# RWKV rebuilt: the triangular inverse as 32x32 tile products on TensorE, keys of two heads formed at 128 partitions, and the old state added by rows of ones in the state's product

## The chip, the cores and the metric

The kernel runs on one core of one Trainium2 chip. The metric is the device time of one execution in microseconds (us). The engines are TensorE (PE, with weight loads shown apart as PEld), VectorE (DVE), ScalarE (ACT) and GpSimd (POOL); SyncE (SP) issues most transfers. A view of the profile shows all of them on one time axis, from the start of the profiled span.

## What is computed

One inference step of a two-layer encoder trunk over 512 prompt tokens and 32 sample tokens, with 1024 features. Both layers have a half SwiGLU, a mixer, cross-attention to 256 memory rows, and another half SwiGLU, each followed by a norm. Layer 0 mixes with a gated linear recurrence and retention, layer 1 with RWKV-7, which is what the change touches: 16 heads of 64, each with a 64x64 state.

```python
def mixer_c(x, shift_buf, s0, mu, w_rkv, w0, w1, w2, a0, a1, a2, g1, g2, k_k, k_a, r_k, gn_g, gn_b, w_out):
    ...
    r, k, v = rkv[0], rkv[1], rkv[2]
    w = -jax.nn.softplus(-(w0 + jnp.tanh(xm[3] @ w1) @ w2)) - 0.5
    decay = jnp.exp(-jnp.exp(w.astype(f32)))
    iclr = jax.nn.sigmoid(a0 + (xm[4] @ a1) @ a2)
    g = jax.nn.sigmoid(xm[5] @ g1) @ g2
    ...
    kk = k * k_k.reshape(RWKV_HEADS, RWKV_HEAD)
    kk = kk / jnp.maximum(jnp.linalg.norm(kk, axis=-1, keepdims=True), 1e-12)
    k = k * (1.0 + (iclr - 1.0) * k_a.reshape(RWKV_HEADS, RWKV_HEAD))

    def step(S, inp):
        r_t, w_t, k_t, v_t, kk_t, b_t = inp
        sa = jnp.einsum('bhvk,bhk->bhv', S, -kk_t)
        S = S * w_t[:, :, None, :] + sa[..., None] * b_t[:, :, None, :] + v_t[..., None] * k_t[:, :, None, :]
        return S, jnp.einsum('bhvk,bhk->bhv', S, r_t)
    ...
    o = layer_norm(o, gn_g..., gn_b..., RWKV_GN_EPS)
    o = o + (r * k * r_k).sum(-1, keepdims=True) * v
    y = (o.reshape(B, T, D).astype(x.dtype) * g) @ w_out
```

## The kernel before

**Layout and linear work.** The whole trunk is one program. Activations lie with features on partitions and tokens in columns, in two halves: A is tokens 0 to 255 of the prompt (256 columns), B is tokens 256 to 511 and the 32 sample tokens (288 columns). Weights stream in as granules of 128 outputs by 8x128 inputs. Each is split into a high part (a copy on ACT) and a low part (a difference on DVE or POOL), and a half's columns are split likewise; a linear granule is then 24 TensorE products of 128x256 or 128x288 (high by high, low by high, high by low). In the trace their operands are called XHA, XLA, HHA, HLA and the same with B for columns, and `W_k` for a slot of split weights, `wr` for a buffer that a load lands in.

**The order of the work.** The parts of the model are Python generators, the tasks. A planner, `Clock`, keeps an estimate of when each engine is free and each operand written. Every helper that issues an instruction (`mm` for a product, `tr` for a transpose, `tt`, `stt`, `_v` for DVE, `gtt` for POOL, `act` for ACT) names a cost to it, and the estimated start becomes the instruction's priority in the scheduler that fixes every engine's queue. `ett` picks the engine, DVE or POOL, that is through first by that estimate. So the numbers in the helpers set the order of the whole program, and no engine's queue is reordered once it is built. A list `SOLO` lets half A run ahead around RWKV, so that A's recurrence stands beside the projections of B, and B's beside A's attention and SwiGLU. A task's band (-1 to -4) puts it ahead of other work.

**The RWKV stage.** `wkv` works on 9 blocks of 64 tokens: four of half A, four of half B and one of 32 sample tokens. A block has two chunks of 32 tokens, the last block one: 17 chunks. Five tasks run side by side.

- `wkv_prep` (band -1) forms per block the decays, the keys and their inverse-decayed forms, then for each chunk and head the product KL'X, 64x64, whose masked result lies in rows 64 to 127 of X. X holds receptance and normalised key (two kinds of 32 columns), KL key and gated key. Both are built for each parity of heads at 64 partitions. The strict triangle N of each head is in X's last 32 rows. The first product of each block's keys is the one with `bonest` 128x512.
- `wkv_solve` (band -2) makes (I + N)^-1 for the 32 heads-and-chunks of a block. N goes by DMA from X to DRAM (`dn<-XHA`, `dn<-W`, one for each chunk) and from there to a tile with one head, chunk and quarter of the rows on each partition (`P<-dn`). Z (part of tile `LC`) starts as the identity; 31 steps of two POOL products each, `P<-LC,P` and `LC<-LC,P`, run on it. Z goes back by DMA (`dz<-LC`, then `W<-dz`) as four-head block-diagonal 128x128 tiles, TB.
- `wkv_load` (band -3) turns KL to tokens-first rows and loads the values' rows into Y.
- `wkv_chain` (band -4) is the recurrence: 16 products over 96 rows, 64 columns (`ax<-wr,W 96*32`), a copy, four products with TB 128x64, copies into Y, 16 products 64x64 of the tokens-first keys with Y, and then on DVE the sum with the old state and the product with the decay; beside it 16 output products of 32 columns (`ax<-XLA,wr 128*64`).
- `wkv_norm` (band -1) is the heads' norm, the bonus and the gate, with four POOL products per block.

The state, DMA staging and scratch live in room that others have left: units of X and KL in the slots XHA, XLA, two weight slots `W_110`/`W_111`, Q1 and P0; N and the step's scratch in P1 (`P_115` in the order, `P` in the profile), TB in a third weight slot (`W_114`). PSUM gives the stage five banks: two to the chain (`ax`), one to load and norm, and two (`pb`, named `mm`) to prep.

The solve's steps, and the end of the chain's state product:

```python
        for s in range(31):
            nr, nt = s // 4 + 1, 31 - s
            T = w.t[:, :nr * nt].rearrange("p (i t) -> p i t", i=nr)
            K.gtt(T, Z[:, :nr, s:s + 1].to_broadcast([128, nr, nt]), N[:, s:s + 1, s + 1:].to_broadcast([128, nr, nt]))
            K.gtt(Z[:, :nr, s + 1:], Z[:, :nr, s + 1:], T, ALU.subtract)
```

## Time and profile before

| | |
|---|---|
| Median of 3 runs | 3024.68 us (3018.31 to 3030.01) |
| Span of the profiled execution | 3028.7 us; the page gives no separate device time for it |
| Granted TensorE clock, mean | 0.945 |
| PE busy | 2833.4 us (94%), 22456 instructions |
| DVE busy | 1743.4 us (58%), 3099 |
| ACT busy | 1276.8 us (42%), 2184 |
| POOL busy | 830.1 us (27%), 1088 |
| Read from HBM | 313.09 MB, 108 GB/s over the span |
| First product of block 0's keys | 1855.97 us |
| End of chunk 7 (half A) and chunk 16 (last) | about 2157 and 2512 us |

How to read it: the share of busy time is a mean over stages with different limits, so the prediction reads it in windows cut at the stage's borders. PE's time includes time at a lowered clock; the windows give the granted clock beside it. One instruction of the program that multiplies in full fp32 leaves two matmul records and two weight loads in the trace, a linear one (in the rounded format) one of each. The chain of waits follows the end of the program back through whatever was waited for last. In a group's row the text before the bar is the operation with its output and inputs and the count, behind it the busy time and the mean of one instruction in ns, then the idle time just before these and what ended it.

### The profile page before, as it was taken

To read this page: it belongs to the slowest core of one execution; us is meant where nothing else is said; L and a number is where in the kernel's file an instruction comes from. 1 tells how busy PE (TensorE), PEld (TensorE's weight loads), DVE (VectorE), ACT (ScalarE), POOL (GpSimd) and SP (SyncE) were. 2 spreads that over 40 slices of the span, in tenths; PEclk is the share of its full clock that TensorE was granted. 3 is DMA by queue.
4 is the path that set the end of the run, shared out by engine and by line. 5 is a ranking of instruction groups with operands and counts; after the bars stand their busy time and mean duration, and the time that the engine had idled before them with its cause. 6 is when DMAs were issued, how large, how long until landed. Compare 5 with 4: busy or idle time off the path is not lost.

```text
span 3028.7 us, 54637 instructions
## 1 busy us (share of the span) xinstructions
PE 2833.4 (94%) x22456; PEld 2716.3 (90%) x22456; DVE 1743.4 (58%) x3099; ACT 1276.8 (42%) x2184; POOL 830.1 (27%) x1088
## 2 busy tenths in 40 slices
PE   9999998998999999999999898888878889999998
PEld 8999998998998999989999897776767779998997
DVE  5333337677767333365355756674675666767655
ACT  4223233665545222234244343343435455655544
POOL 2001104333313000032011212466375543422301
PEclk9999999999999999999999998788778879999999
DMA  6443443322332232322356453122223135645563
GB/s 182 126 119 115 130 119 97 88 68 81 98 98 84 85 90 84 89 87 77 90 155 179 120 168 106 39 65 62 69 73 87 49 98 174 177 141 157 169 176 93
DMA packets 626331, 330.56 MB, mean 109 GB/s; under 512 B 45480, under 2 KB 620160, under 8 KB 626080
## 3 DMA queue, kind: packets, MB, share of 16 engines
q1 hardware_dynamic: 617952, 317.06, 36.8%
q0 software_dynamic: 3488, 9.44, 1.0%
q8 instruction: 176, 2.88, 0.4%
q10 hardware_dynamic: 4640, 0.56, 0.1%
q14 instruction: 75, 0.61, 0.1%
HBM read 313.09 MB, written 13.92 MB: 108 GB/s over the span
## 4 chain that ended last, share of the span: by engine, by line
PE 66%; DVE 10%; POOL 9%; DMA 7%; ACT 5%; issue 3%; SPq 0%; ACTq 0%; DVEq 0%; POOLq 0%
PE mm L395 60%; PE ax L395 4%; POOL LC L412 3%; POOL P L412 3%; DMA P<-dn 3%; DVE W L408 2%; ACT arena L486 1%; ACT W L486 1%; DVE arena L408 1%; DMA wr<-in_ffn_up 1%; PE ax L400 1%; DVE arena L432 1%; POOL arena L412 1%; ACT L2049 1%; DVE XB L408 1%
## 5 line engine op out<-in xcount | busy, mean ns | idle before, releaser
L486 ACT ACTIVATE W<-wr 128x1024 fp32r<-128x1024 f32 (+1 forms) x558 | 577.0, 1038 | 737.4 <-PE mm L395 560.0
L408 DVE TENSOR_TENSOR W<-wr,W 128x1024 fp32r<-128x1024 f32 (+1 forms) x455 | 561.5, 1236 | 551.7 <-ACT W L486 542.8
L395 PE MATMUL mm<-XHB,W 128*128 128x288 f32 x3840 | 585.1, 302 | 14.1 <-ACT XHB L486 4.7
L395 PE MATMUL mm<-XHA,W 128*128 128x256 f32 x3840 | 538.4, 290 | 28.9 <-ACT XHA L486 11.6
L395 PEld LDWEIGHTS mm<-XHB,W 128*128 128x128 f32 x3840 | 532.4, 191 | 25.0 <-ACT XHB L486 5.8
L395 PEld LDWEIGHTS mm<-XHA,W 128*128 128x128 f32 x3840 | 499.7, 194 | 39.7 <-ACT XHA L486 16.0
L412 POOL TENSOR_TENSOR W<-wr,W 128x1024 fp32r<-128x1024 f32 (+1 forms) x103 | 251.0, 2439 | 606.2 <-ACT W L486 550.6
L395 PE MATMUL mm<-XLB,W 128*128 128x288 f32 x1984 | 318.7, 300 | 0.7 <-DVE XLB L408 0.7
L395 PE MATMUL mm<-HHB,W 128*128 128x288 f32 x1920 | 291.0, 301 | 11.4 <-ACT W L486 4.4
L395 PEld LDWEIGHTS mm<-XLB,W 128*128 128x128 f32 x1984 | 283.0, 190 | 3.2 <-DVE XLB L408 1.1
L395 PE MATMUL mm<-XLA,W 128*128 128x256 f32 x1984 | 284.7, 283 | 0.0
L395 PEld LDWEIGHTS mm<-HHB,W 128*128 128x128 f32 x1920 | 267.0, 191 | 15.0 <-ACT W L486 5.3
L395 PE MATMUL mm<-HHA,W 128*128 128x256 f32 x1920 | 265.7, 288 | 5.9 <-POOL W L412 2.2
L395 PEld LDWEIGHTS mm<-XLA,W 128*128 128x128 f32 x1984 | 259.1, 190 | 0.3 <-DVE XLA L408 0.2
L395 PEld LDWEIGHTS mm<-HHA,W 128*128 128x128 f32 x1920 | 247.1, 192 | 8.8 <-POOL W L412 2.6
L486 ACT ACTIVATE arena<-mm 128x256 f32<-128x256 f32 (+4 forms) x292 | 112.2, 387 | 305.1 <-PE mm L395 287.5
L432 DVE SCALAR_TENSOR_TENSOR arena<-mm,arena 128x288 f32<-128x288 f32 (+1 forms) x176 | 77.2, 439 | 157.7 <-PE mm L395 149.0
L395 PE MATMUL mm<-HLB,W 128*128 128x288 f32 x896 | 144.3, 301 | 0.3 <-DVE HLB L408 0.3
L412 POOL TENSOR_TENSOR P<-LC,P 128x66 f32<-128x66 f32 (+24 forms) x279 | 113.5, 407 | 84.6 <-DMA P<-dn 64.6
L395 PEld LDWEIGHTS mm<-HLB,W 128*128 128x128 f32 x896 | 130.1, 193 | 0.6 <-DVE HLB L408 0.5
L395 PE MATMUL mm<-HLA,W 128*128 128x256 f32 x896 | 129.3, 284 | 0.0
L412 POOL TENSOR_TENSOR LC<-LC,P 128x66 f32<-128x66 f32 (+24 forms) x279 | 115.0, 412 | 20.5
(426 smaller groups left out, 3612.0 us busy)
## 6 DMA issues: line engine op xcount, KB each, us to landing
wr<-in_ffn_up SPq DMA_DIRECT2D x246, 512.0 KB
wr<-in_ffn_down SPq DMA_DIRECT2D x96, 448.0 KB
wr<-in_l_w_rkv SPq DMA_DIRECT2D x48, 512.0 KB
wr<-in_ffn_down SPq DMA_DIRECT2D x40, 512.0 KB
wr<-in_l_w_in SPq DMA_DIRECT2D x24, 512.0 KB
wr<-in_l_w_out SPq DMA_DIRECT2D x24, 512.0 KB
wr<-in_xa_q SPq DMA_DIRECT2D x24, 512.0 KB
wr<-in_xa_o SPq DMA_DIRECT2D x24, 512.0 KB
```

The source lines that it names most:

```text
L395: self.nc.tensor.matmul(out, lhsT, rhs, start=start, stop=stop)
L400: self.nc.tensor.transpose(out, in_, self.ident[k0:k0 + k, k0:k0 + k])
L408: self.nc.vector.tensor_tensor(out, a, b, op=op)
L412: self.nc.gpsimd.tensor_tensor(out, a, b, op=op)
L432: self.nc.vector.scalar_tensor_tensor(out, a, s, b, op0=op0, op1=op1)
L486: return self.nc.scalar.activation(out, a, f, bias=bias, scale=scale, **kw)
L2049: nc.scalar.preload_act_table_set(name)
```

## The change

- **Inverse.** `wkv_solve` no longer uses POOL and DRAM. N is split by masks into the parts within tiles of 8 rows (d and its transpose dt), within 16 but not 8 (et) and the rest (ft). The inverse of the 8-row part is (I-d)(I+d2)(I+d4) by products, and the two larger parts are taken in by two more steps. All of it is eleven times 32 (16 in the last block) products of 32x32 by 32x32, four of them side by side in the four 32-row, 32-column quadrants of the array, with six evictions to SBUF by ACT and DVE between them. It takes its two PSUM banks from the same pair as prep (`w.ps = w.pb`). N and its transpose come from 64 products of 32x32 over 64 rows (`mm<-W 32x32 x64` below).
- **Keys.** X and KL of both chunks of a block are formed at 128 partitions at once, two heads of a pair on the two halves of the partitions. The key products run two side by side (two 64x64 quadrants). ACT copies the odd heads' keys to the lower partitions.
- **State.** The tokens-first keys have their own buffers, KT, with the identity in rows 0 to 63, so that the state's product over 128 rows adds the old state; the DVE sum goes.
- **TB** is applied as 16 products of 32x64 per chunk instead of four of 128x64, and has three buffers, so that the solve may be three blocks ahead of the chain (two before).
- **POOL to DVE.** The product with `k_k` in prep and four products and sums per block in the norm change from `gtt` to `tt`. In the norm the copy of the centred rows by ACT goes and its second PSUM bank comes from `pb`. Prep takes its two gate banks one after the other.
- **Planner.** The costs in `mm`, `_v`, `gtt`, `ett`, `gmemset`, `scan` and `act` have other numbers; `mm` has an argument `side`, how many products stand side by side. The priorities of the whole program come from these.
- Room: Q1 and P0 are given back at the start; blocks take XHA and XLA (half A), then XHB and XLB. Comments are taken out.

```diff
@@ class Kern
-    def mm(self, out, lhsT, rhs, start=True, stop=True):
+    def mm(self, out, lhsT, rhs, start=True, stop=True, side=1):
         n = free_size(rhs)
+        m = out.shape[0]
         if lhsT.dtype == F32R:
-            cost = (n if n >= 256 else max(4 * n, 128)) / 2.4 + 2
+            cost = n / 2.4 + 13 if n >= 256 else max(4 * n / 2.4, m / 1.2) + 2
+        elif m > 64 and side == 1:
+            cost = max(4 * n / 2.4, 2 * m / 1.2) + 15
         else:
-            cost = 4 * (max(n, 62) / 2.4) + 2
+            cost = (4 * n / 2.4 + 2 * m / 1.2) / side + 2
...
-        self.plan("v", 70 + free_size(out) / (1.92 if fast else 0.96), [out], ins)
+        self.plan("v", 147 + free_size(out) / (1.92 if fast else 0.96), [out], ins)
...
-        self.plan("g", 150 + free_size(out) * 2.0, [out], [a, b])
+        self.plan("g", 190 + free_size(out) * 2.1, [out], [a, b])
...
-        dur = (60 if a.space == PSUM else 100) + free_size(out) / 1.2
+        dur = (165 if a.space == PSUM else 204) + free_size(out) / 1.2
@@ wkv_norm
-        K.act(o, p3)
...
-        K.gtt(o, o, q)
-        K.gtt(o, o, bv(K.gng2))
+        K.tt(o, p3, q)
+        K.tt(o, o, bv(K.gng2))
...
@@ wkv
+    for t in w.kt:
+        K.vcopy(t[0:64], K.ident[0:64, None, 0:64].to_broadcast([64, 16, 64]))
+    K.qt.give("Q1", "P0")
...
+    w.ps = w.pb
@@ wkv_prep
-        K.gtt(a4, k, vb("k_k"))
+        K.tt(a4, k, vb("k_k"))
...
+        tx, X = yield from w.units.take()
+        KL = w.kl[b] = yield from w.kls.take()
...
+        K.tt(kb[:, 0], by(k), by(Pv))
+        K.tt(kb[:, 1], by(a3), by(Pv))
+        K.tt(xv[:, 0, 0], by(r), by(P))
+        K.tt(xv[:, 0, 1, :, :, 1:32], by(kk)[:, :, :, 1:32], by(P)[:, :, :, 0:31])
+        K.vcopy(xv[:, 0, 1, :, :, 0], by(kk)[:, :, :, 0])
+        yield lambda: b == 0 or event(K, "cut", b - 1).set
+        ps = yield from w.pb.take()
+        up, lo = cut(ps[:, :256]), cut(ps[:, 256:])
+        for out, x, y in ((up, KL, X), (lo, X, KL)):
+            ...
+                    K.mm(out[32 * q:32 * q + 32, 4 * c + g], x1, y1, side=4)
+        K.tt(dt, up, mk(0))
+        K.tt(d, lo, mk(1))
+        K.tt(et, up, mk(2))
+        K.tt(ft, up, mk(3))
+        event(K, "kb", b).fire(K)
...
-            K.dma(w.dn[b % 2][c].rearrange("h s t -> s h t"), X[96:128, :, 32:64])
...
@@ wkv_solve
-        yield lambda: b < 2 or event(K, "chain", b - 2).set
+        yield lambda: b < 3 or event(K, "chain", b - 3).set
...
+        def product(out, left, right):
+            for g in range(4 * nch):
+                for q in range(4):
+                    u = slice(32 * q, 32 * q + 32)
+                    K.mm(out[u, g], left[u, g], right[u, g], side=4)
+        K.tt(idt, dt, m(4), ALU.add)
+        ps, p, pt = yield from bank()
+        product(p, dt, d)
+        product(pt, d, dt)
+        K.act(d2, both)
+        K.tt(id2, p, m(4), ALU.add)
+        ...
+        ps, p, pt = yield from bank()
+        product(p, et, t8[:, 0])
+        K.tt(iw, m(4), p, ALU.subtract)
+        ...
+        product(p, iw2, t16[:, 1])
+        event(K, "cut", b).fire(K)
+        K.act(cut(w.tb[b % 3]), p)
@@ wkv_chain
-            K.mm(pu[:, g * 64:g * 64 + 64], TB[:, 4 * c + g], RS[:, g])
+            for q in range(4):
+                u = slice(32 * q, 32 * q + 32)
+                K.mm(pu[u, g * 64:g * 64 + 64], TB[u, 4 * c + g], RS[u, g], side=4)
...
-            K.mm(b1[64 * q:64 * q + 64, g * 64:g * 64 + 64], KL[64:128, 8 * q + g], Y[64:128, 8 * q + g])
+            K.mm(b1[64 * q:64 * q + 64, g * 64:g * 64 + 64], KT[:, 8 * q + g], Y[:, 8 * q + g], side=2)
...
-            K.tt(yn, b1[64 * q:64 * q + 64].rearrange("p (g v) -> p g v", g=8), Y[0:64, 8 * q:8 * q + 8], ALU.add)
-            K.tt(yn, yn, pc[:, 8 * q:8 * q + 8, None].to_broadcast([64, 8, 64]))
+            K.tt(yn, b1[64 * q:64 * q + 64].rearrange("p (g v) -> p g v", g=8),
+                 pc[:, 8 * q:8 * q + 8, None].to_broadcast([64, 8, 64]))
```

Counted over the whole program (one for each instruction): products on PE 20846 to 24586, of them 3536 new of 32x32; POOL 1093 to 458; DVE 3101 to 3056; ACT 2164 to 2202; SP 737 to 679. From the first `bonest` 128x512 to the last output product, neighbours on PE with another array shape are 343 before and 535 after.

Three places in the order. A row is the line of a helper, the operation, output and inputs by tile names with numbers, the output's shape, and a count of neighbours that read alike.

First, SP's queue at block 0, before: the triangle N of two chunks goes out, comes back, and the inverse goes out and comes back.

```order
L491 DMA wr_77<-in_l_w_rkv 128x8x128
L491 DMA dn_17680<-XHA_17670 32x16x32
L491 DMA dn_17680<-XLA_17671 32x16x32
L491 DMA P_115_17677<-dn_17680 128x1x1024
L491 DMA dz_17682<-LC_7380 4x256x32
L491 DMA W_114_17676<-dz_17682 32x8x32 x2
```

After, SP has no such rows; a constant, the masks, is loaded earlier, with the low-rank weights:

```order
L501 DMA LC_7380<-in_c_wmask 128x64
L501 DMA LC_7380<-in_c_winv 128x160
L501 DMA LC_7380<-in_c_sgn 128x1
```

What moved: five transfers per block are gone from SP's queue, which now holds loads of weights alone while blocks are solved.

Second, POOL's queue at block 0, before: the norm of half B's columns (`XB`, `arena`) and then the first of 31 pairs of the inverse (62 rows follow one another, for 31, 30, 29 and so on elements).

```order
L412 TENSOR_TENSOR XB_98<-XB_98,arena_79 128x288
L412 TENSOR_TENSOR P_115_17677<-LC_7380,P_115_17677 128x31
L412 TENSOR_TENSOR LC_7380<-LC_7380,P_115_17677 128x31
L412 TENSOR_TENSOR P_115_17677<-LC_7380,P_115_17677 128x30
L412 TENSOR_TENSOR LC_7380<-LC_7380,P_115_17677 128x30
```

After, behind the same norm row:

```order
L422 TENSOR_TENSOR XB_98<-XB_98,arena_79 128x288
L422 TENSOR_TENSOR W_1_71<-wr_76,W_1_71 128x1024
L422 TENSOR_TENSOR W_4_74<-wr_77,W_4_74 128x1024 x2
L422 TENSOR_TENSOR W_1_71<-wr_76,W_1_71 128x1024
```

What moved: the pairs are gone, and splits of weights (`W<-wr,W`) stand there.

Third, PE's queue around a chunk of half A and the next block's keys, before: TB is applied (`ax_68<-arena_79,W_114`), the next chunk's key products are issued in eights, and linear products of half B (`mm<-XHB`, `mm<-XLB`) lie between.

```order
L395 MATMUL mm_63<-XLB_100,W_4_74 128x288 x8
L395 MATMUL mm_65<-XHB_99,W_3_73 128x288
L395 MATMUL ax_68<-arena_79,W_114_17676 128x64 x4
L395 MATMUL mm_64<-W_111_17673 64x64 x8
L395 MATMUL mm_66<-W_111_17673 64x64 x8
L395 MATMUL mm_65<-XHB_99,W_3_73 128x288 x15
L395 MATMUL mm_65<-XLB_100,W_3_73 128x288 x8
L395 MATMUL mm_64<-arena_79,bonest 128x512
```

After, a like place: the triangles of a block (`mm_63<-W_112 32x32 x64`), products of the solve (32x32 between `P_113` and `W_112`), a chunk's first products (`ax_67<-Q_114,XHA`), the gate's (`mm_64<-SUMA,LC`), transposes, and linear products of half B's SwiGLU (`HHB`, `HLB`: the hidden columns, split).

```order
L405 MATMUL mm_63<-W_112_17555 32x32 x64
L410 MATMUL ax_70<-identt,VA_16400 32x128 x2
L405 MATMUL mm_64<-arena_79,bonest 128x512
L405 MATMUL mm_65<-HHB_13223,W_4_74 128x288 x8
L405 MATMUL mm_65<-HLB_13224,W_4_74 128x288 x7
L405 MATMUL mm_63<-P_113_17556,W_112_17555 32x32 x32
L410 MATMUL ax_70<-identt,VA_16400 32x128 x4
L405 MATMUL mm_64<-SUMA_16263,LC_7380 128x64 x8
L405 MATMUL ax_67<-Q_114_17557,XHA_17549 32x64 x16
L405 MATMUL mm_63<-W_112_17555,P_113_17556 32x32 x32
```

What moved: the solve's steps now stand in PE's own queue, in bursts of 32 or 64 between linear pieces of 7 to 16 products, and the work that lies between them is another part of half B than before.

232 lines of the change are left out of this document (128 added, 104 removed).

## The prediction

> **What bounds the kernel now.** I read the windows first, cut at the borders of the RWKV stage: from the first product with `bonest` 128x512 (the start of block 0's keys) to the last output product of chunk 7 (the end of half A's recurrence), of chunk 8 (B's first) and of chunk 16 (B's last).
>
> ```profile
> 0.00:1856.00 1856.00, 1792.52 (x13895) 1766.82 (x13896) 975.65 (x1813) 727.17 (x1253) 345.01 (x319) 0.98 0.38 110
> 1856.00:2157.00 301.00, 252.65 (x2138) 211.56 (x2138) 203.53 (x362) 125.25 (x226) 164.71 (x307) 0.82 0.25 60
> 2157.00:2243.00 86.00, 75.37 (x589) 64.37 (x585) 61.36 (x112) 34.90 (x61) 44.92 (x87) 0.76 0.29 74
> 2243.00:2512.00 269.00, 221.41 (x2056) 191.07 (x2055) 170.10 (x320) 124.27 (x236) 147.80 (x295) 0.81 0.28 77
> 2512.00:3028.00 516.00, 491.44 (x3793) 482.44 (x3789) 332.75 (x496) 265.16 (x409) 127.61 (x82) 0.98 0.54 155
> ...
> 480.00:970.00 490.00, 452.94 (x3399) 437.81 (x3399) 355.05 (x907) 268.89 (x544) 175.22 (x175) 0.96 0.29 84
> ```
>
> The columns are the stretch and its length, then busy us and count of PE, weight loads, DVE, ACT and POOL, then the granted clock, DMA share and GB/s. Outside the stage PE is busy 96% at clock 0.98: those 2372 us only get shorter if PE gets less to do. Inside it (656 us) the granted clock is 0.76 to 0.82 and every engine has idle time, so something in series sets the pace. The chain of waits over 1856 to 2512 names it; its pieces follow.
>
> ```profile
> by line: PE mm L395 19.4%; POOL LC L412 13.4%; POOL P L412 13.2%; DMA P<-dn 13.0%; issue 6.1%; PE ax L395 5.8%; POOL HLA L412 2.7%; DVE W L408 2.6%; DMA dn<-W 2.3%; PE ax L400 2.2%; DMA dz<-LC 2.2%; ACT arena L486 1.6%; POOL W L412 1.5%; DV
> ...
> 1900.68 9.14 DMA P<-dn
> ...
> 1959.40 11.23 DMA P<-dn
> 2003.57 4.89 DMA dz<-LC
> 2012.06 9.82 DMA P<-dn
> ...
> 2071.76 12.19 DMA P<-dn
> ```
>
> POOL LC and P (the 31 steps of the inverse) with the transfers P<-dn, dn<-W and dz<-LC are 44% of the chain, some 290 us. The rows in order of time give the pace: a block's P<-dn starts 59, 53 and 60 us after the one before. The next view takes the nine stretches in which POOL runs the inverse (first, last, and the sum of all nine, with the instructions on LC alone):
>
> ```profile
> 1909.50:1940.20 30.70, 0.46 (x5) 0.32 (x3) 1.21 (x1) 0.00 (x0) 25.53 (x62) 0.91 0.00 1
> ...
> 2442.20:2474.40 32.20, 2.85 (x14) 2.65 (x13) 0.00 (x0) 1.36 (x2) 23.84 (x62) 0.82 0.13 37
> sum 315.40, PE 19.70 PEld 17.64 DVE 14.80 ACT 12.28 POOL 226.14; mean PE 2.19 PEld 1.96 DVE 1.65 ACT 1.36 POOL 25.13
> ```
>
> Nine inverses take 315 us of POOL time, 35 each; with 9 to 12 us of loading, 5 of storing and the read back, the loop of one block is some 50 us. So the recurrence is bound by `wkv_solve`, with the making of the keys close behind.
>
> **The change, part by part.** *1. The inverse goes to TensorE.* Removed: 558 POOL products, 46 memsets, 41 DMA issues on SP for dn, P and dz, and 36 more on SP and ACT that read the inverse back. Added per full block: 64 products 32x32 over 64 rows (the two triangles) and eleven times 32 products 32x32, each followed by an eviction. A product is two records. No 32x32 product with 32 columns in a burst stands in the trace; the nearest rows are the 96*32 ones with 64 columns, four at a time in four column strips, then the pairs and the singles of 64*64:
>
> ```profile
> 2030.13:2030.36 0.23, 0.22 (x16) 0.22 (x16) 0.00 (x0) 0.00 (x0) 0.00 (x0) 1.00 0.00 0
> 2335.56:2335.90 0.34, 0.34 (x15) 0.34 (x17) 0.00 (x0) 0.00 (x0) 0.00 (x0) 0.50 0.19 50
> ...
> L395 PE MATMUL ax<-wr,W 96*32 96x64 f32 (+1 forms) x256 | 11.0, 264 | 3.6 <-ACT HLB L486 2.1 <-DVE wr L443 0.9 <-DVE wr L408 0.7
> L395 PE MATMUL mm<-W 64*64 64x64 f32 x256 | 30.0, 287 | 8.5 <-DVE W L408 8.5
> L395 PE MATMUL ax<-Q,XHB 64*64 64x64 f32 (+1 forms) x128 | 6.9, 285 | 0.5 <-ACT Q L486 0.5
> L408 DVE TENSOR_TENSOR arena<-mm,LC 128x256 f32<-128x256 f32 (+1 forms) x16 | 6.9, 432 | 3.4 <-ACT arena L486 3.3
> L486 ACT ACTIVATE W<-ax,LC 64x512 f32<-64x512 f32 x16 | 10.9, 682 | 0.4 <-PE ax L400 0.2
> ```
>
> Sixteen records take 0.23 us at clock 1.00, 14 ns each, and fifteen 0.34 at clock 0.50, 23 ns; the group over all bursts, with tails and half clock, 43. Half the columns can at best halve the 14 to 7. I take 10 ns a record, 20 a product, nearer the full-clock row since the new bursts are long, and keep 7 and 43 for the range. With 3536 products in the whole stage that is 71 us of PE (50 to 304).
>
> The length of one inverse: eleven bursts of 64 records at 14 ns (the higher price, since a burst here ends before its eviction starts) are 9.9 us; seven banks' tails of 0.26 are 1.8; evictions in series are one DVE at 0.43, three ACT at 0.68, three DVE at 0.43 and a last one about the same, 4.2. With the triangles (1.8 us) and their four masks (4 x 0.43) it makes 19.5 us; in company I take 25, against about 50 now.
>
> The Trainium skill, "TensorE: Matmul & The Clock Gate", section "Wait — 56ns, not 53.3ns?", speaks against this part: it says that matmuls never start less than about 25 ns apart, however few their columns. The row of 16 records at 14 ns does not bear that out for neighbours in different column strips, so the sum goes by the row; by the page's figure the new products would be an estimated 177 us instead of 71, and the time about 2980 (third rival).
>
> *2. Keys of two heads at 128 partitions.* Sixteen DVE products of 64x256 and eight copies per block become four products of 128x512 and one copy:
>
> ```profile
> L408 DVE TENSOR_TENSOR W<-HHB,arena 64x256 f32<-64x256 f32 x10 | 6.3, 635 | 0.2
> L408 DVE TENSOR_TENSOR arena<-arena,pv 128x512 f32<-128x512 f32 (+1 forms) x9 | 6.2, 684 | 0.1
> L408 DVE TENSOR_TENSOR wr<-ax,Q 64x512 f32<-64x512 f32 x18 | 12.4, 686 | 4.3 <-PE ax L395 4.0
> L412 POOL TENSOR_TENSOR HLB<-HLB,HHB 128x512 f32<-128x512 f32 (+1 forms) x5 | 7.2, 1446 | 0.3
> 2062.84 0.47 PE L395 MATMUL mm<-W 64*64 64x64 f32 x2
> 2063.24 0.61 PE L395 MATMUL mm<-XLB,W 128*128 128x288 f32 x1
> 2063.78 0.69 PE L395 MATMUL mm<-W 64*64 64x64 f32 x4
> ```
>
> That is 10.2 us down to 2.7 of DVE a block. The key products run in pairs: 54 instead of 117 ns a record by the two 64*64 rows above, at full clock about half as much, so 15 us of PE come back in all. Against it ACT copies half of each chunk's keys (17 x 0.68 = 12 us, in ACT's idle time: 125 of 301 us busy in half A's window).
>
> *3. Old state by ones in the product.* The add on DVE goes, two of 0.686 a chunk, 23 us in all, 1.4 us of it a chunk on the recurrence itself. The product reads 128 rows instead of 64 at the same columns, which costs PE nothing by its rows.
>
> *4. POOL's work in norm and keys to DVE.* 45 products of about 1.4 us on POOL become 45 of 0.684 on DVE, +31 us; DVE gains the masks and identities (nine of 0.43 a block, 33 us) and loses 64 (part 2) and 23. DVE stays at about 180 us in half A, no bound.
>
> *5. Order.* The planner's costs change, so all queues are reordered. PE's order now changes array shape 192 times more within the stage (535 against 343). In the three rows at half clock a pair of records and a linear product take 0.94 us together where 0.24 and some 0.23 would do: 0.23 a change, 0.12 at full clock; I take 0.1, 20 us. What it does to the waits before 1856 I cost at nothing, with 20 us either way in the range.
>
> **The sum.** The price of linear work is one row of the chain:
>
> ```profile
> 88.85 14.99 PE mm L395 x120
> ...
> 1855.97 0.59 PE L395 MATMUL mm<-arena,bonest 128*128 128x512 f32 x1
> 1898.92 0.33 SPq L491 DMA_DIRECT2D dn<-XLA  x1
> 1997.38 1.13 PE L395 MATMUL ax<-XLA,wr 128*64 128x32 f32 x32
> 2156.68 1.12 PE L395 MATMUL ax<-W,wr 128*64 128x32 f32 x32
> ```
>
> 0.125 us each. By the programs' own orders the three stretches hold 633, 198 and 775 linear and attention products before, 444, 917 and 571 after; 93 come out of the stretch before the stage and 233 out of the one behind it, since A's output and attention now run while B's projections are still being made. The other fp32 products I price at 0.11 us (two records, around the pair row). PE's load before: 79+91, 25+23, 97+80 = 170, 48 and 177 us in 301, 86 and 269. After:
> - half A: 170 - 24 (linear) + 33 (1664 small products) - 7 (pairs) + 5 (45 changes) = 177
> - between: 48 + 90 + 10 - 1 + 4 = 151
> - half B: 177 - 26 + 28 - 7 + 11 = 183
>
> Then the waits. Block 0's keys take 43 us (1855.97 to 1898.92), which was hidden by 50 us of inverse and comes out now: per block I take 48, the keys with some queueing, against 53 from chunk 1's end (1998.5) to chunk 7's (2157.8). Half A: 43 keys + 25 inverse + 14 for two chunks + 3 x 48 = 226 (load 177, 78%). Between: 103 us of PE work stand in the order before B's first triangles, then keys, inverse and a chunk, 75: 178. Half B: 7 + 3 x 48 + 35 for the short block = 186 by latency, but 183 of PE load at the 88% that a well-filled stretch reaches gives 208, and I take that. Before the stage 1856 - 12 = 1844, behind it 516.7 - 28 = 489. 1844 + 226 + 178 + 208 + 489 = 2945, against the profiled span of 3028.7. The page gives no other time of that execution; the median of the runs, 3024.68, is 4 below its span, so I forecast 2941, 2.8% faster.
>
> **The rivals.**
> *Waits vanish.* PE becomes dense in the stage, the clock goes to 1.00. For it: the window 480 to 970, with its many chains, has PE busy 92% at 0.96. At 92% the loads become 192, 164 and 199: 1844+555+489-4 = 2884. Against it: one bank pair serves keys, norm and inverse. Chance 0.18.
> *The inverse was covered.* If the keys set the 53 to 60 us between blocks, that pace stays: 43+25+14+3x57 = 253, 190, 230: 3002. For it: dn of a block is issued just before its P<-dn (1898.92 and 1900.68). Against it: keys made on POOL's queue behind the inverse were held by it. Chance 0.20, a third of it within half a per cent.
> *Small products are dear* (slower). At 43 ns a record, as the 96*32 group shows, PE's load in the three stretches grows by 110, 32 and 92 to 287, 183 and 275; at 95% that is 784: 1844+784+489-4 = 3113. It decides from about 31 ns a record, where the stage is as long as now. The floor of 25 ns gives 511+106 = 617, 649 at 95%: 2980. For it: half clock at 23 ns and 64 records between two evictions. Against: 14 ns in the row. Chance 0.07 for more than 31 ns, 0.05 for about 25.
>
> **Numbers.** The forecast (2900 to 2985) has 0.50, the four cases above 0.18, 0.20, 0.07 and 0.05. The range runs from the first rival with 20 us of gain before the stage to just above the second: 2865 to 3010. A measurement here can tell about half a per cent from nothing (15 us). Faster 0.87, same 0.06, slower 0.07.
>
> **What would show it.** The distance between blocks should fall to 45 to 50 us, chunk 7 should end 220 to 235 us after the first `bonest` product, no DMA and no POOL product should stand in the chain between two blocks, and POOL should be busy under 100 us in the stage. The group of 32x32 products should show 7 to 14 ns a record at full clock. PE's clock in the stage should be 0.85 or more. I am wrong if the pace stays above 55 us, if the small products stand one after another, or if the stretch before the stage moves by more than 20 us.

## The result: 4.0% slower, and where the profile after shows it

The changed kernel takes 3145.05 us (median of 4 runs, 3140.92 to 3146.76) against 3025.66 us of the kernel before beside it: a ratio of 1.0401, 95% interval 1.0383 to 1.0419. The forecast was 2941.

The windows of the changed kernel, cut at the same borders as before (first `bonest` 128x512 product, end of chunk 7, of chunk 8, of chunk 16); the columns are those of the prediction's first fence.

```profile
0.00:1858.30 1858.30, 1787.03 (x13818) 1760.18 (x13818) 974.14 (x1802) 724.86 (x1248) 349.78 (x316) 0.98 0.38 109
1858.30:2148.40 290.10, 248.98 (x5440) 201.30 (x5439) 166.08 (x296) 121.13 (x217) 33.47 (x19) 0.85 0.14 38
2148.40:2362.60 214.20, 180.10 (x2257) 162.16 (x2260) 141.27 (x239) 98.46 (x178) 39.21 (x26) 0.90 0.33 94
2362.60:2640.00 277.40, 239.83 (x4909) 197.86 (x4908) 140.19 (x248) 124.45 (x210) 25.28 (x12) 0.83 0.20 58
2640.00:3142.90 502.90, 472.70 (x3524) 462.31 (x3524) 308.91 (x470) 245.63 (x387) 120.82 (x80) 0.95 0.50 145
```

| | before | forecast | after |
|---|---|---|---|
| ahead of the stage | 1856 | 1844 | 1858 |
| half A | 302 | 226 | 290 |
| between the halves | 87 | 178 | 214 |
| half B | 268 | 208 | 277 |
| behind | 516 | 489 | 503 |

GpSimd is out of the stage, as meant (98 us of busy time in it instead of 357), and the granted clock there rose from 0.76-0.82 to 0.83-0.90. Yet half A is only 12 us shorter and half B 9 us longer. Multiplying PE's busy time in each window by its clock splits the span in three: work at full clock, time lost to the lowered clock, and idle. Before: about 2682 + 151 + 195. After: about 2773 + 155 + 214. TensorE has some 90 us more to do (84 if the clock is taken over the busy time alone, from the trace's clock records, and not over the whole windows), and none of the microseconds that the prediction meant to win from clock and waits came back.

The chain of waits over the stage after, by line:

```profile
by line: PE mm L405 34.2%; PE ax L405 14.3%; issue 7.8%; ACT arena L496 5.2%; PE ax L410 4.6%; DVE arena L418 4.4%; ACT W L496 3.3%; DVE W L418 3.3%; DVE arena L442 2.9%; ACT L2123 1.3%; DVE XLB L418 1.2%; DMA wr<-in_l_w_rkv 1.1%; DVE arena
```

The 44% of GpSimd and of transfers between two blocks are gone. TensorE's own lines have taken their place: 53% (34.2 + 14.3 + 4.6) instead of 27% (19.4 + 5.8 + 2.2). The 32x32 products themselves, by group in the stage (busy us, mean ns of one, which overlaps its neighbours), and one burst of 130 records in a window of its own:

```profile
L405 PE MATMUL mm<-W 32*32 32x32 f32 x2720 | 38.9, 199 | 3.9 <-issue 3.9
L405 PE MATMUL mm<-P,W 32*32 32x32 f32 x2176 | 30.5, 203 | 13.0 <-DVE W L418 10.2 <-ACT P L496 2.4 <-issue 0.3
L405 PE MATMUL mm<-P 32*32 32x32 f32 x544 | 8.0, 197 | 0.8 <-issue 0.8
L405 PE MATMUL mm<-W,P 32*32 32x32 f32 x544 | 6.5, 194 | 1.0 <-DVE W L418 1.0
...
1980.15:1981.46 1.31, 1.31 (x130) 1.00 0.00 0
```

In a burst a record takes 10 ns at clock 1.00, the forecast's price to the digit; with tails and half clock the four groups are 14 (83.9 us for 5984). So the products look as cheap as forecast. The experiments overturn that.

How long an inverse takes shows in the order of time. The middle steps of block 1's inverse, from the timeline: PE's bursts of 32x32 products, some of what stands between them, and the evictions on ScalarE and VectorE (start, length in us):

```profile
1980.15 1.29 PE L405 MATMUL mm<-W 32*32 32x32 f32 x128
...
1981.37 2.00 PE L405 MATMUL mm<-SUMA,LC 64*128 64x64 f32 x16
1981.66 0.59 ACT L496 ACTIVATE P<-mm 128x512 f32<-128x512 f32 x1
...
1985.91 2.00 PE L405 MATMUL mm<-SUMA,LC 64*128 64x64 f32 x16
...
1987.84 0.75 PE L405 MATMUL mm<-P,W 32*32 32x32 f32 x64
...
1991.74 0.41 DVE L418 TENSOR_TENSOR W<-LC,mm 128x256 f32<-128x256 f32 x1
...
1992.94 0.72 PE L405 MATMUL mm<-W,P 32*32 32x32 f32 x62
...
1993.52 0.71 PE L405 MATMUL mm<-P,W 32*32 32x32 f32 x62
...
1999.83 0.58 ACT L496 ACTIVATE P<-mm 128x512 f32<-128x512 f32 x1
...
2000.46 1.08 PE L405 MATMUL mm<-P,W 32*32 32x32 f32 x64 [2.06 <-ACT P L496]
...
2003.21 2.00 DVE L418 TENSOR_TENSOR HLA<-HLA,gng 128x512 f32<-128x512 f32 x1
...
2005.25 0.69 DVE L418 TENSOR_TENSOR HLA<-HLA,HHA 128x512 f32<-128x512 f32 x1
...
2005.86 0.41 DVE L418 TENSOR_TENSOR W<-LC,mm 128x256 f32<-128x256 f32 x1
```

A burst of 1.3 us is ready for its eviction at once, but the next burst stands behind 5.6 us of other products in PE's queue (1982.25 to 1987.84), the eviction after that 3.2 us behind other work on VectorE (to 1991.74), the next 5.6 us on ScalarE, the last behind the norm's products (`HLA`) that the change had moved to VectorE. From the first triangle to TB the eight full blocks take 47 to 83 us, 60 in the mean, where the forecast had 25 and the GpSimd loop some 50. The next block's triangles follow the last product of an inverse within 4 us in all seven cases within a half; in half A they come 56, 73 and 47 us apart. So the inverse, as long as this, may itself set the distance between blocks. No run here settles it: none made the inverse shorter without taking work off TensorE.

### The profile page after: what moved, and what is told of

The parts are those of the page before. It is cut to its first block, busy times and chain, and to the rows that moved or that the text cites. A ratio compares the mean times of both kernels' runs of the same rounds, so it can differ in the third digit from the quotient of the medians.

```text
span 3142.9 us, 68842 instructions
## 1 busy us (share of the span) xinstructions
PE 2928.6 (93%) x29936; PEld 2783.8 (89%) x29936; DVE 1730.6 (55%) x3054; ACT 1314.5 (42%) x2240; POOL 568.6 (18%) x453
## 3 DMA queue, kind: packets, MB, share of 16 engines
q8 instruction: 234, 3.83, 0.5%
## 4 chain that ended last, share of the span: by engine, by line
PE 74%; DVE 12%; ACT 6%; issue 3%; DMA 2%; POOL 2%; SPq 0%; ACTq 0%; DVEq 0%; POOLq 0%
PE mm L405 66%; PE ax L405 6%; DVE arena L418 2%; ACT arena L496 2%; PE ax L410 2%; DVE W L418 2%; ACT W L496 2%; DVE XA L418 1%; DVE arena L442 1%; DVE XB L418 1%; ACT L2123 1%; POOL arena L422 1%; POOL XA L422 1%; POOL XB L422 1%; DVE P L418 0%
## 5 line engine op out<-in xcount | busy, mean ns | idle before, releaser
L405 PE MATMUL mm<-XHB,W 128*128 128x288 f32 (+2 forms) x4160 | 584.5, 294 | 17.0 <-DVE W L418 5.9
L405 PE MATMUL mm<-XHA,W 128*128 128x256 f32 (+2 forms) x4096 | 556.1, 288 | 32.6 <-ACT XHA L496 12.7
L405 PEld LDWEIGHTS mm<-XHB,W 128*128 128x128 f32 (+2 forms) x4160 | 537.4, 186 | 24.4 <-DVE W L418 6.9
L405 PEld LDWEIGHTS mm<-XHA,W 128*128 128x128 f32 (+2 forms) x4096 | 510.3, 192 | 49.8 <-ACT XHA L496 17.3
L405 PE MATMUL mm<-XLB,W 128*128 128x288 f32 (+2 forms) x2240 | 323.7, 290 | 2.7 <-issue 1.2
L405 PE MATMUL mm<-XLA,W 128*128 128x256 f32 (+2 forms) x2240 | 299.6, 281 | 0.5 <-DVE XLA L418 0.3
L405 PEld LDWEIGHTS mm<-XLB,W 128*128 128x128 f32 (+2 forms) x2240 | 288.5, 183 | 5.5 <-issue 3.6
L405 PEld LDWEIGHTS mm<-XLA,W 128*128 128x128 f32 (+2 forms) x2240 | 269.3, 187 | 5.3 <-issue 3.1
L418 DVE TENSOR_TENSOR arena<-arena 128x256 f32<-128x256 f32 (+3 forms) x137 | 98.6, 722 | 46.6 <-ACT arena L496 44.6
L405 PEld LDWEIGHTS mm<-HLA,W 128*128 128x128 f32 x896 | 118.4, 191 | 1.1
```

Source lines behind the costliest of these rows:

```text
L405: self.nc.tensor.matmul(out, lhsT, rhs, start=start, stop=stop)
L418: self.nc.vector.tensor_tensor(out, a, b, op=op)
```

## The experiments

Each ran beside the kernel before on one chip; times are medians, ratios those to the kernel before with their 95% interval. "Theory Q" in the expectations is the first theory after the result: the inverse's steps in TensorE's own queue, by their load or by their series waits. Rival O is the new order of the program, rival K the new making of the keys.

**1. What each part is worth.** First the planner's costs alone, on the kernel before:

```diff
-            cost = 4 * (max(n, 62) / 2.4) + 2
+            cost = (4 * n / 2.4 + 2 * m / 1.2) / side + 2
...
...
-        self.plan("v", 70 + free_size(out) / (1.92 if fast else 0.96), [out], ins)
+        self.plan("v", 147 + free_size(out) / (1.92 if fast else 0.96), [out], ins)
```

and the same for the other numbers of the change's planner part (`gtt`, `ett`, `gmemset`, `scan`, `act`).

> The kernel before with the planner's new costs alone (and the `side` argument at the same calls). Theory Q (the inverse's steps stand in TensorE's own queue behind linear pieces, and add some 84 us of 32x32 products to the engine that is busy 93% of the span): the costs matter little, 3025 plus or minus 20 us. Rival O (the new costs reorder the program: 444 linear products beside half A's recurrence instead of 633, 917 instead of 198 between the halves): most of the loss of 119 us comes with them, 3085 to 3145 us, and the stretch between chunk 7 and chunk 8 grows from 87 us to over 150.

Measured 3065.43 us, 1.0137 (1.0121 to 1.0154). Neither theory's number: the costs matter, but they are a third of the loss. Between chunk 7 and chunk 8 lie 102 us, not 150. The stretches of this kernel and of the next ones, in us:

| kernel | ahead | half A | between | half B | behind |
|---|---|---|---|---|---|
| before | 1856 | 302 | 87 | 268 | 516 |
| before, new costs | 1851 | 326 | 102 | 262 | 523 |
| before, new costs of `mm` alone | 1884 | 316 | 73 | 230 | 564 |
| changed | 1858 | 290 | 214 | 277 | 503 |
| changed, old costs | 1859 | 265 | 238 | 202 | 522 |
| changed, GpSimd inverse | 1851 | 296 | 165 | 252 | 510 |
| the same, old costs | 1857 | 284 | 145 | 256 | 509 |

> The kernel before with the new costs of TensorE's products alone, those of VectorE, ScalarE and GpSimd left old. If the 43 us of the new costs come from the longer vector and scalar costs (the planner then believes these engines late and puts linear work elsewhere): 3022 plus or minus 10 us. If they come from TensorE's: 3055 to 3070 us.

Measured 3069.86 us, 1.0162 (1.0147 to 1.0177): with the costs of `mm` alone a loss of the same size is there, and those of the other engines, about twice as high for short instructions, add nothing to it. It lies elsewhere, though. With all new costs the stage grows from 657 us to 690. Here the stage itself is shorter (619 us), but it begins 28 us later and has 564 us behind it instead of 516: beside half B's recurrence stand 548 linear products instead of 776, the others come after it.

> The changed kernel with the planner's old costs. Theory Q: 3145 plus or minus 25 us, the inverse of a block still takes 47 to 70 us from its triangles to its last product. Rival O: the loss goes with the new costs, 3025 to 3070 us, and the stretch between the halves shrinks from 214 us to about 100.

Measured 3089.9 us, 1.0220 (1.0202 to 1.0238): 55 us less than the changed kernel, so the costs are worth 43 us from one side and 55 from the other. In this kernel half A takes 265 us and half B 202, near the forecast's 226 and 208; but 238 us lie between the halves.

The inverse as a part, taken back to GpSimd with everything else changed (the 31 steps and the transfers of the old `wkv_solve`, into the new TB layout):

> The changed kernel with the old inverse (31 steps on GpSimd, through DRAM) in place of the tile products; keys, state, norm, room and costs stay changed, and the triangles and the wait of a block's triangles for the inverse before it go. Theory Q: TensorE loses the 84 us of 32x32 products and their waits, 3010 to 3050 us. Rival O: the order stays bad, 3100 or more. Rival K (the new making of keys and its shared banks set the pace): blocks stay 60 us or more apart in half A, 3100 or more.

Measured 3082.44 us, 1.0190 (1.0172 to 1.0209): the tile inverse costs 63 us under the new costs. With the old costs as well:

> The changed keys, state, norm and room, with the old GpSimd inverse and the planner's old costs. If the loss is the sum of the planner's costs (43 to 55 us) and the inverse (63 us) and little else: 3082 - 43 to 55 = 3027 to 3039 us. If the new keys, state and room have a cost of their own that the new costs hid: over 3050. If they are a gain that the costs hid: under 3015.

Measured 3054.38 us, 1.0113 (1.0098 to 1.0129). That is over the 3050 at which the new keys, state, norm and room have a cost of their own: 33 us against the kernel before, 17 under the new costs. So three parts lose: the costs 28 to 55 (28 with the GpSimd inverse, 3082 against 3054), the tile inverse 36 to 63, the rest 17 to 33. In the table the rest's loss lies between the halves, where every kernel with the new room has 145 us or more.

**2. What a 32x32 product costs in place.** Eight of the eleven products of each inverse left out, and the planner told so:

```diff
-        product(p, d2[:, 1], d2[:, 0])
-        product(pt, id2, idt)
...
-        product(p, iw2, t16[:, 1])
+        product(p, id2, idt)
```

> The changed kernel with 3 of the inverse's 11 products and one wait kept; 8 products and 5 of its evictions in series are left out, so TB is not the inverse. Theory Q: 8/11 of the 32x32 products go (about 55 us of TensorE) and the pace is no longer set by the inverse: 3145 - 55 - 20 to 40 = 3050 to 3070 us, blocks of half A under 50 us apart. Rival O: only the load goes, 3090 to 3110. Rival K: blocks stay over 60 us apart, 3090 or more.

Measured 3034.3 us, 1.0036 (1.0023 to 1.0049): 111 us less than the changed kernel, more than any theory gave. Load or waits? All products kept, their operands changed to tiles that are ready at once:

```diff
-        product(p, d2[:, 1], d2[:, 0])
-        product(pt, id2, idt)
+        product(p, et, ft)
+        product(pt, ft, et)
...
-        product(p, iw2, t16[:, 1])
+        product(p, idt, idt)
```

> The changed kernel with all eleven products and all seven evictions of each inverse kept in number and shape, but the products after the first bank read the masked triangles, which are ready at once, so that no product waits for an eviction of the one before it (TB is then not the inverse). TensorE's work is the same to the instruction. Theory Q in its form 'series' (the waits between the steps, some 34 us of a block's 60 in the changed kernel's trace, set the pace): 3065 to 3110 us, triangles to TB 30 us or less. Theory Q in its form 'load' (the 32x32 products cost what they cost TensorE, the waits are filled by linear work): 3145 plus or minus 15 us.

Measured 3158.04 us, 1.0458 (1.0415 to 1.0501). No faster; but the edit did not make the inverse shorter either. In this run's trace the eight full blocks take 41 to 89 us from the first triangle to the last product, 56 in the mean (46 to 83 and 60 without the edit), where the theory of series waits expected 30 or less. Block 1, from its first triangles to its last burst, which an eviction of other work (`DVE arena`) releases:

```profile
1931.21 1.08 PE L405 MATMUL mm<-XLA,W 64*32 64x32 f32 x64 [1.50 <-DVE W L418]
...
1996.26 0.75 PE L405 MATMUL mm<-W 32*32 32x32 f32 x64 [3.74 <-DVE arena L442]
```

So it is not its own evictions that make an inverse long; without that dependence the bursts stand about as far apart in PE's queue. What a shorter inverse would be worth the run does not show. The price of the products themselves, first by leaving products out while the planner goes on booking them, so that the order hardly moves:

```diff
+                    if g % every == 0:
                         K.mm(out[u, g], left[u, g], right[u, g], side=4)
+                    else:
+                        K.plan("pe", (4 * 32 / 2.4 + 2 * 32 / 1.2) / 4 + 2, [out[u, g]], [left[u, g], right[u, g]])
```

> The changed kernel with ten of the inverse's eleven products issued only for one column tile of each eight (4 of 32 products; the last one whole, on the first step's operand), while the planner goes on booking all of them: 2360 of 2992 products are left out, and evictions, waits and the plan stay (TB is then not the inverse). It prices a 32x32 product in place. At the 10 ns a record of an undisturbed burst: 4720 records, 47 us less, 3098 us. At 14 ns (the mean busy time in the stage): 3079. At 25 ns (what the run with eight products fewer would give if its 111 us were all theirs): 3027. If linear work or waits fill the freed time: 3145.

Measured 3031.05 us, 1.0017 (1.0007 to 1.0028): 114 us for 2360 products, 48 ns each, 24 a record. Then by issuing each twice:

```diff
                     K.mm(out[u, g], left[u, g], right[u, g], side=4)
+                    K.nc.tensor.matmul(out[u, g], left[u, g], right[u, g], start=True, stop=True)
```

> The changed kernel with each 32x32 product of the inverse issued twice in a row into the same place, the second over the first (the planner books one): 2992 more products, nothing else. At 10 ns a record 60 us more, 3205; at 14 ns 3229; at 25 ns 3295. If TensorE's idle time in the stage (113 us) takes them: 3145 to 3160.

Measured 3319.0 us, 1.0967 (1.0948 to 1.0986): 174 us for 2992 products, 58 ns each, 29 a record. The same three windows of the stage, thinned and then doubled:

```profile
1852.50:2095.50 243.00, 207.91 (x3200) 168.88 (x3199) 167.72 (x295) 120.78 (x217) 31.18 (x20) 0.89 0.16 44
2095.50:2297.50 202.00, 170.99 (x1654) 154.15 (x1652) 135.92 (x236) 96.06 (x173) 33.36 (x23) 0.90 0.33 97
2297.50:2523.30 225.80, 199.03 (x3028) 168.04 (x3028) 143.00 (x251) 129.68 (x219) 23.56 (x14) 0.87 0.25 70
```

```profile
1854.10:2228.00 373.90, 317.70 (x8256) 258.08 (x8255) 170.39 (x296) 122.14 (x217) 28.99 (x19) 0.78 0.11 31
2228.00:2462.10 234.10, 199.28 (x2942) 180.45 (x2942) 138.32 (x239) 98.10 (x178) 36.83 (x26) 0.86 0.30 87
2462.10:2813.30 351.20, 309.85 (x7387) 253.49 (x7387) 141.69 (x248) 124.46 (x210) 24.46 (x12) 0.77 0.17 47
```

The stage is 671, 782 and 959 us long with the same 1996 linear products in it, 508, some 920 and some 570 in the three windows. Counted from each record's start to the next one's with idle time taken out, the 111 us from thinned to changed are: the small products' own time 53 (34 to 87, 12 ns a record), the linear products 21 (309 to 330, though none was added), the other products 17, and idle time 20. From changed to doubled: 90, 44, 23 and 20. So about half of the price in place is own time. Some third is longer neighbours, the rest idle time. The clock falls meanwhile, as the windows show: 0.89/0.90/0.87, then 0.85/0.90/0.83, then 0.78/0.86/0.77. Split by the trace's clock records over the whole program, the 115 us between the profiled spans of thinned and changed are 53 of work at full clock, 46 lost to the lowered clock and 15 idle; the 173 from changed to doubled are 76, 74 and 23. The inverse also changes its length with its products, 44, 60 and 79 us in the mean from the first triangle to the last product, so these two runs do not tell load on TensorE from the length of the inverse. Nor does any run say why taking the whole tile inverse back to GpSimd wins 36 to 63 us and leaving most of its products out 114.

Was the inverse on GpSimd the bound of the kernel before? 27 of its 31 steps are left out, the planner booking them as ever:

```diff
+            if s >= 4:
+                K.plan("g", 150 + nr * nt * 2.0, [T], [Z[:, :nr, s:s + 1], N[:, s:s + 1, s + 1:]])
+                K.plan("g", 150 + nr * nt * 2.0, [Z[:, :nr, s + 1:]], [Z[:, :nr, s + 1:], T])
+                continue
             K.gtt(T, Z[:, :nr, s:s + 1]..., N[:, s:s + 1, s + 1:]...)
```

> The kernel before with 4 of the inverse's 31 steps issued on GpSimd, while the planner goes on booking all 31 (TB is then not the inverse). It tests the prediction's first premise: that the inverse on GpSimd sets the pace of the blocks. Premise right: a block's loop falls from some 50 to 30 us, the keys set the pace at 45 to 48: 3022 - 8 x 5 to 20 = 2860 to 2980 us. Premise wrong, TensorE's queue and load set the pace and GpSimd's steps are covered: 3005 to 3025 us.

Measured 2999.35 us, 0.9908 (0.9893 to 0.9923): 27 us. The stage and the chain of waits over it:

```profile
1853.30:2136.60 283.30, 252.05 (x2119) 208.50 (x2117) 198.09 (x361) 122.89 (x224) 67.91 (x91) 0.83 0.24 62
2136.60:2216.30 79.70, 64.59 (x571) 57.05 (x572) 60.29 (x103) 32.13 (x56) 23.57 (x28) 0.85 0.29 80
2216.30:2480.90 264.60, 224.87 (x2140) 195.85 (x2138) 177.78 (x331) 131.67 (x246) 69.77 (x83) 0.83 0.31 82
...
by line: PE mm L395 22.0%; DMA P<-dn 11.3%; PE ax L395 7.8%; DVE W L408 5.9%; DMA dz<-LC 4.7%; issue 3.8%; DVE arena L432 2.9%; DVE arena L408 2.9%; ACT arena L486 2.5%; PE ax L400 2.4%; DVE XLB L408 2.3%; DMA wr<-in_ffn_up 2.2%; DMA dn<-W 
```

GpSimd's steps had 27% of the chain, some 175 us of it; with nearly all of them gone, the stage is 30 us shorter, PE is as busy as before in it (541 us against 549), and half A still takes 283. The distance between blocks, which the prediction read from the starts of `P<-dn` (59, 53 and 60 us), did not follow. On the queue of SP:

```profile
1898.01 0.63 SPq L491 DMA_DIRECT2D P<-dn  x1
1911.54 0.54 SPq L491 DMA_DIRECT2D dz<-LC  x1
...
1951.70 0.55 SPq L491 DMA_DIRECT2D P<-dn  x1
1967.00 0.55 SPq L491 DMA_DIRECT2D dz<-LC  x1
...
2004.25 0.54 SPq L491 DMA_DIRECT2D P<-dn  x1
2019.99 0.52 SPq L491 DMA_DIRECT2D dz<-LC  x1
...
2060.32 0.54 SPq L491 DMA_DIRECT2D P<-dn  x1
2076.50 0.55 SPq L491 DMA_DIRECT2D dz<-LC  x1
```

From `P<-dn` to `dz<-LC` a block takes 14 to 16 us now and took 40 to 48 before, and yet the blocks come 54, 53 and 56 us apart. The inverse was covered. The chain of waits named what was waited for last, not what the time would be without it. With the plan made for the short inverse it is no better:

> As the run before, but the planner too books 4 steps, so that the whole program is ordered for a short inverse. If only the plan kept the freed time from being used: clearly under that run, by 30 us or more. If the order is not what holds it: within 25 us of that run either way. The other side of the premise: over 3040 us would say that the plan for a shorter inverse is itself the worse one.

Measured 3017.74 us, 0.9974 (0.9963 to 0.9984), 18 us more than with the wrong plan.

And is there room on TensorE in the kernel before? The same number of 32x32 products added, ahead of each group of key products:

```diff
                 ps = yield from w.pb.take()
+                for z in range(88):
+                    r2, k2, g = z % 2, z % 2, z // 2 % 8
+                    K.nc.tensor.matmul(ps[64 + 32 * k2:96 + 32 * k2, g * 64:g * 64 + 32], KL[...], X[...], start=True, stop=True)
                 for g in range(8):
```

> The kernel before with 2992 extra 32x32 products, 88 ahead of each group of eight key products, into the bank that these then write over; nobody waits for them but the key products behind them, and the planner does not book them. If TensorE's time sets the stage of the kernel before as well, they cost what they cost in the changed kernel, 24 to 29 ns a record: 3022 + 144 to 174 = 3165 to 3195 us. If the stage of the kernel before has room on TensorE (259 us by the load at full clock), as the prediction had it: under 3080.

Measured 3234.87 us, 1.0694 (1.0677 to 1.0710): 209 us, 70 ns a product, with the clock in the stage down to 0.73 to 0.80. None of it was hidden: the products' own time, counted as above, is 143 us (24 ns a record; they go to two quadrants in turn, the inverse's to four). So the 259 us that a sum at full clock left free could not be used at this place. That the stage is full is not shown by it, because the keys, on which the blocks wait, stand right behind these products. The chain of waits in the stage goes through them (L1856) and still through GpSimd's inverse:

```profile
by line: PE mm L395 23.2%; PE mm L1856 13.3%; PE ax L395 11.1%; POOL P L412 11.1%; POOL LC L412 10.4%; DMA P<-dn 7.3%; issue 4.9%; PE ax L400 2.8%; DMA dz<-LC 2.7%; POOL W L412 1.5%; DVE W L408 1.2%; ACT arena L486 1.2%; DMA dn<-W 1.1%; DVE
```

**3. Order and the other parts.** Half B's first triangles come 150 us after half A's end in the changed kernel (2299.9 us against 2148.4), where the forecast had 103. Half B's projections put first once half A's recurrence is through:

```diff
         for j in range(8):
+            if isb and event(K, "chain", 3).set:
+                K.task[7] = K.band = -1
             ps = yield from K.linear(h, h.xh, h.xl)
```

> The changed kernel with half B's projections put first in the same way. Late start: 3145 - 30 to 60 = 3085 to 3115 us. TensorE's load alone: 3145 plus or minus 15 us.

Measured 3107.77 us, 1.0272 (1.0257 to 1.0288): 37 us won; the middle is 194 us instead of 214, half B 259 instead of 277. The late start is part of the loss here. Not so with the GpSimd inverse:

> The changed keys, state, norm and room with the old GpSimd inverse and the old costs (3054 us), and half B's projections put ahead of half A's attention once half A's recurrence has ended. If the loss of 33 us against the kernel before is half B's late start (145 us between the halves against 87): 3015 to 3035 us, the stretch under 110. If the stretch is filled by TensorE work that has to be done anyway: 3045 to 3065.

Measured 3061.14 us, 1.0119 (1.0104 to 1.0135), 7 us more than without it, and 147 us between the halves as before.

The norm's work (three of its four products of a block, and `k_k`) back on GpSimd in the changed kernel, and then all of it moved to VectorE in the kernel before (`gtt` to `tt`, nothing else):

> The changed kernel with three of the four norm products of a block and the product with k_k back on GpSimd. If the inverse's evictions wait behind them on VectorE (the evictions wait 11 us of a block's 60): a block's inverse is 3 to 6 us shorter, 3115 to 3135 us. If VectorE is no matter, since TensorE's load decides: 3145 plus or minus 12 us; if the norm's slower products delay the half's end: up to 3160.

Measured 3130.76 us, 1.0368 (1.0351 to 1.0386): 14 us won. The inverse's wait for evictions did not fall (100 us over eight blocks, 92 before the edit), so the reason given is not the one.

> The kernel before with the norm's four products of a block and the product with k_k on VectorE in place of GpSimd, nothing else. By the run with them back on GpSimd (14 us faster): VectorE, with more readers waiting on it, is the worse place, 3025 to 3045. If GpSimd's queue, in which they stood behind the inverse, was the worse place: 3000 to 3015.

Measured 3104.21 us, 1.0264 (1.0245 to 1.0283): 78 us lost to 45 instructions that changed engine, 2.5 times what they take. Half A grew by 20 us, the middle by 54, and idle time of PE in the stage from 107 to 143. How much of it is VectorE, and how much the new order that follows from any change, was to be told by putting the good parts together. The keys, the state and the room alone:

> The changed keys, state and room alone: the old GpSimd inverse, the old costs, and three of the norm's products of a block and the product with k_k on GpSimd as before. If the norm on VectorE is a loss by itself (78 us in the kernel before, 14 in the changed one): 3054 - 14 to 78 = 2976 to 3040 us, and under 3015 it would beat both kernels. If the 78 us were an accident of that order: 3045 to 3065.

Measured 3064.51 us, 1.0134 (1.0113 to 1.0154): no gain from the norm on GpSimd here, 10 us more than with it on VectorE. And the tile inverse with three repairs that won 55, 14 and 37 us alone:

> The changed kernel with the tile inverse, and three repairs together: the old costs (55 us by themselves), the norm's three products and k_k on GpSimd (14 us), half B's projections first after half A's recurrence (37 us). If they add up: 3145 - 106 = 3039 us. If the order decides anew each time: 3060 to 3100. Under 3010 it would beat the kernel before.

Measured 3105.7 us, 1.0260 (1.0236 to 1.0284), where the sum of the three would be 3039: more than with the old costs alone (3089.9). Effects of 10 to 80 us, of edits that move the plan, did not add up in these runs. No version tried that computes the whole beats the kernel before.

## Why the prediction was wrong

**The step that failed first: "So the recurrence is bound by `wkv_solve`", and with it "Then the waits".** The prediction priced TensorE's work at full clock (about 400 us in a stage of 656) and took what was left for waits that the inverse on GpSimd caused, to be filled to 78% and 88% afterwards. It read the bound from the chain's 44%. With 27 of the 31 steps gone the blocks still came 54, 53 and 56 us apart, and the kernel won 27 us, where 84 had been forecast from the whole change. Its own first fence gave a warning: PE was busy 84% of that stage (549.4 of 656 us), at clock 0.8. In the short-inverse run the clock rose only from 0.76-0.82 to 0.83-0.85: most of the lowered clock stayed when the steps of the inverse went.

**The term mis-sized: the price of a small product.** 20 ns in the sum (71 us for 3536). In a burst it is 20 (130 records in 1.31 us). In place it is 48 (thinned), 58 (doubled) and 70 (added before). 2992 products at 48 to 58 are 144 to 174 us, of which the sum had 60. The prediction kept a range up to 86 ns a product, but gave over 62 a chance of 0.07 and the 50 of the floor 0.05, and held both against a base that had the waits won already. The Trainium skill, "TensorE: Matmul & The Clock Gate", section "Wait — 56ns, not 53.3ns?", had a start-to-start floor of about 25 ns for each matmul. As a spacing the trace contradicts it again (10 ns in the burst of 130). As the price of one record more in this program, 24 and 29 ns come out near it; by the page's figure the 4720 records left out would be an estimated 118 us, and the run gave 114. That is luck as far as these runs show: about half of the 24 is the record's own time, the rest longer neighbours and idle time.

**"The length of one inverse ... in company I take 25".** It took 47 to 83 us. By the prediction's own sum half A was 43 + 3 x 48 + 25 + 14 = 226. It came out as 23 to the first triangles, 175 from there to the fourth block's, 51 for the last inverse and 41 for the chunks behind it, 290 in all. How much the length of the inverse costs by itself stays open: the run without its series waits (3158 us) left it as long as before.

**"The planner's costs change, so all queues are reordered ... 20 us".** Alone they cost 43 us, and the new price of a product in `mm` is enough for it. It is not through array shapes (by the records, 355 changes between neighbours in the stage before, 343 with the new costs). That it is through where linear work comes to lie is argued from the stretches, not shown.

**Right:** GpSimd's busy time in the stage (98 us, under 100), the chain without `P`, `LC` and `dn`, the clock at about 0.85 (0.83 to 0.90), the spacing of records in a burst, the stretch ahead of the stage within 20 us of 1856 (though 14 us above 1844: 93 linear products fewer did not shorten it). TensorE's added work, 84 to 91 us at full clock, is near the 75 us of the prediction's own loads (511 - 395, less 326 linear products moved in at 0.125).

**The distance between blocks.** Chunks 1, 3, 5 and 7 end 73, 65 and 39 us apart after (59 in the mean, above the 55 that the prediction named as a sign of being wrong), 55, 62 and 42 before; 45 to 50 had been forecast. On the inverse in the kernel before, the second rival, "The inverse was covered", was the right one; it had a chance of 0.20. But the prediction held its rivals one at a time, and here the covered inverse and the dear product came together. What sets half A's length, 265 to 326 us in all kernels but those with products thinned, doubled or added, is not shown. Products on TensorE move it (243 us thinned, 374 doubled), a shorter inverse on GpSimd moves it little (283 against 302). In the changed kernel it can be the load on TensorE or the length of the inverse in its queue, and no run tells the two apart. Open too is the part of the 17 to 33 us of the new keys, state and room that is theirs and not that of the order.

## What to carry to other kernels

Where an engine is busy 84% at a lowered clock, do not count its remaining time as won. Take the supposed bound away first and see whether the time falls: that run is cheap, and here it contradicted the chain of waits. Add dummy work too and see whether it is hidden, but away from the path in question, or a longer path looks like a full engine. When an edit is meant to take a wait away, look in the trace whether the wait is gone before reading the time. Price a small instruction by leaving it out of the program in place, not by its spacing in a burst: here its own time was about half of the price. Where a planner orders the whole program, the effect of an edit under some 3% can be that of a new order as much as of the edit, and edits that win alone do not add up.

## What the runs showed of the hardware

TensorE seems to run out of instructions at times. In the doubled kernel 75 us of PE's waits in the stage have no releaser but "issue" (12 in the changed kernel, 3 in the thinned one). One of these holes and the clock around it (PE busy and count, clock, DMA share, GB/s):

```profile
2019.00:2019.54 0.54, 0.54 (x55) 1.00 0.17 30
2019.54:2021.74 2.20, 0.00 (x0) 0.95 0.00 0
2021.74:2022.74 1.00, 0.99 (x58) 0.50 0.00 0
```

The transfers from 2019.00 to 2021.74, with the one packet at about 2019.1:

```profile
DMA packets 1, 0.02 MB, mean 6 GB/s; under 512 B 0, under 2 KB 0, under 8 KB 0
## 3 DMA queue, kind: packets, MB, share of 16 engines
q8 instruction: 1, 0.02, 3.3%
```

PE stops in the midst of a burst with nothing to wait for, and goes on 2.6 us after the start of a packet on the queue of instructions. All 31 such holes of over 0.5 us inside bursts of the doubled kernel's stage end 2.3 to 2.9 us after such a packet began; with 145 of these packets in the 959 us of the stage, chance would have it so for about one in eleven. The program needs 176 of these packets before, 234 after, 281 doubled (2.88, 3.83 and 4.60 MB). Behind this hole the clock is 0.50. It is not so at once behind each: in the half microsecond behind them, 9 of the 31 holes have half clock. But where the clock was full in the microsecond before a hole, it falls within 5 us behind it in 25 of 26 cases, while of all instants with a full clock in this stage 38% are followed by a fall as soon. In all these traces the clock records are whole multiples of 3.41 us long, so a fall can come some time after its cause. The Trainium skill, "TensorE: Matmul & The Clock Gate", section "What's actually happening", puts the fall to half clock behind an idle window of about 3.4 us; here it fell behind 2.2 us of emptiness. That the clock loss of the linear products in the doubled kernel comes from such holes is argued from these counts; how much of it does was not measured.
